# A decoder layer on one core: the input projection's twelve blocks in five groups, and w_o begun from its GLA half

## The chip, the core and the metric

The kernel runs on one core of one Trainium2 chip. The metric is device time in microseconds (us), the median of the runs shown; one profiled execution gives the trace. Five engines work side by side: TensorE (PE in the rows, with its weight loads as PEld), VectorE (DVE), ScalarE (ACT), GpSimd (POOL) and SyncE (SP), which here only issues the weight transfers.

## The reference

One layer, batch 1, 256 positions, width 2048, all in float32:

```python
c_act = jax.nn.silu(c)
mod = (c_act @ w_ada[l] + b_ada[l])[:, None, :]
sh1, sc1, gt1, sh2, sc2, gt2 = jnp.split(mod, N_MOD, axis=-1)
h = rms_norm(x, g_mix_norm[l]) * (1.0 + sc1) + sh1
proj = h @ w_in[l]
dq, dk, dv, gq, gk, gv, gg, g_low = jnp.split(proj, PROJ_SPLITS, axis=-1)
...
mix = jnp.concatenate([od, og], axis=-1) @ w_o[l]
x = x + gt1 * mix
h2 = rms_norm(x, g_ffn_norm[l]) * (1.0 + sc2) + sh2
u, g = jnp.split(h2 @ w_up[l], 2, axis=-1)
act = jax.nn.gelu(causal_dwconv(g, w_conv[l], b_conv[l]), approximate=False) * u
x = x + gt2 * (act @ w_down[l])
return rms_norm(x, g_final)
```

Between `proj` and `mix` stand two head groups: differential attention (DA, 8 heads, from dq, dk, dv) gives `od`, and gated linear attention (GLA, 4 heads, from gq, gk, gv, gg, with decays from g_low) gives `og`.

## The kernel before

**The stream of weights.** Every weight is read once, by SP, in transfers of 512 KB. A unit (`load_unit`, L97) is two k tiles of 128 rows by 512 columns: one transfer into a `raw` buffer, a rounding copy `wh` on ACT (L110), the remainder `wl` on DVE (L111). TensorE then does three products per tile, since float32 is made of two parts. `b_block` (L114) has the weights stationary, 24 matmuls of 256 columns per unit (recorded under L129); `a_block` (L149) has the activations stationary, 12 matmuls of 512 columns per unit (L163). There are five `raw` buffers, three `wh` and three `wl`.

**The modulation.** `c_act @ w_ada` is a product with one row. `ada_gen` (L207) loads w_ada through the same `raw` buffers (name `raw_a`), multiplies on DVE (`acc`, L241), adds up over partitions on TensorE (`ps_mod`, L221) and yields after each transfer. The generators wait in a list `bg`. Each `load_unit` adds `rate[0]` to a credit and takes one step of the list for every whole credit; `drain` takes steps until a named generator is done. In the list stand sh1 and sc1 (name ada1, eight generators of two k tiles each), then gt1, then sh2 and sc2 (ada2_0 to ada2_3), then gt2.

**The input projection.** Its 12 blocks of 512 columns are gk, gq, gv0, gv1, gg0, gg1, dq0, dk0, dv0 and dq1, dk1, dv1. The first nine are computed in groups of k tiles, `KGROUPS = (2, 4, 4, 6)`, since only those k tiles of h whose ada1 is done can be used: each group opens a block in PSUM (L723; a partial sum is copied back in by ACT, L726), adds its k tiles and closes it by an ACT copy (L731). `need` (L669) drains ada1 and forms h (`norm_T`) just ahead of the block that wants it. The last three blocks, `LATER`, run afterwards over all 16 k tiles at once. PSUM has two slots for blocks.

**The heads.** GLA and DA are generators too, in a second list `fg` with credits of its own, stepped by the units (`frate`). GLA starts behind gv1 of the last group, DA of heads 0 to 3 (`da(0)`) runs within LATER, DA of heads 4 to 7 (`da(1)`) within w_o.

**The output projection and beyond.** w_o has four blocks of 512 columns (nb). nb 0 and 1 take the GLA half of their rows first, then the DA rows; nb 2 and 3 take all rows. Then `drain("ada2_0")` (L818), the second norm, and the up projection in groups (4, 4, 8) of k tiles, seven of its eleven chunks spilled between groups. Then the down projection.

**The order.** The kernel is built with a scheduler that sorts each engine's instructions by a modelled timeline, within their dependences; engines and queues then run in that order.

Of the kernel before, what the change touches and what calls it, by code (L numbers as in the profile page):

```python
# [20 lines left out]
KGROUPS = (2, 4, 4, 6)  # L21
# [25 lines left out]
def tile_decoder_layer(  # L47
# [13 lines left out]
    RAW, WH, WL = 5, 3, 3  # L61
# [13 lines left out]
    fg, fcredit, frate = [], [0.0], [0.0]  # L75

# [20 lines left out]
    def load_unit(view, kt, c0):  # L97
# [8 lines left out]
        raw = stage.tile([P, 2, 512], F32, tag="raw", name="raw", bufs=RAW)  # L106
# [100 lines left out]
    def ada_gen(segs, width, c0, finish, psp, on_pe=(), by_rows=False):  # L207
# [122 lines left out]

    def setup_consts():
        dlam = t1.tile([P, 6, 64], F32, tag="w4", name="dlam", bufs=3)
        dl2 = dlam[:, 4:6]
# [23 lines left out]
        for h in range(DA_HEADS):  # L357
            V.tensor_scalar(identh[:, h], ident, 2.0 ** -(h + 1) / DA_SCALE, None, op0=ALU.mult)

        for l in range(NLEV + 2):  # L360
# [21 lines left out]
            V.tensor_copy(cmat[:, l], cf)  # L382

        for l in range(NLEV):
            h = 1 << l
# [281 lines left out]
    hT = []  # L667

    def need(kts):  # L669

        while len(hT) <= kts[-1]:
            k = len(hT)
            drain(ada1[k])
            hT.extend(norm_T(t1, rst1, s1, sh1, k, f"hT{k}", 1 if k == 0 else 2))

    def in_block(bi, ps, kts, first, last):
        n, c0, tr = BLOCKS[bi]
        need(kts)
        (b_block if tr else a_block)(ps, w_in_v, c0, kts, hT, first, last)
        if bi != 1:  # L680
            return
        if kts[0] == 0:
            setup_consts()
        pl = pss.tile([P, 512], F32, tag="ms", name="ps_low")
        for k in kts:
# [297 lines left out]
```

## Time and profile before

| | |
|---|---|
| median of 3 runs | 1324.97 us (1324.36 to 1326.58) |
| the profiled execution, its own time | 1323.78 us |
| its span in the trace | 1322.1 us |
| TensorE busy | 1247.1 us (94%), 8492 matmuls |
| VectorE busy | 898.2 us (68%) |
| ScalarE busy | 701.4 us (53%) |
| moved by DMA | 314.59 MB, mean 238 GB/s |

A busy TensorE is not one at its peak: a matmul's record is longer than the distance to the next one. So the work done in a stretch is counted by matmuls and their distance where they follow each other without a gap, and the rest of the stretch is loss.

### The profile page before, as it was taken

What the parts mean: (1) busy time and instruction counts of PE and PEld (TensorE: products, weight loads), DVE (VectorE), ACT (ScalarE), POOL (GpSimd) and SP (SyncE); (2) the same over time, 40 slices, a digit from 0 to 9 for tenths busy, and PEclk for the clock granted to TensorE, in tenths of its full rate; (3) what the DMA queues carried; (4) which work ended last, traced back from release to release, by engine and by line L of the source; (5) the groups of instructions that cost most, each with busy time, mean ns of one, the idle gap of its engine ahead of it and who ended that gap; (6) DMA issues with size and microseconds to landing.
All of it is one profiled execution on the core that took longest, in us unless ns stands there. A gap on an engine that the chain in (4) does not pass through costs nothing.

```text
span 1322.1 us, 21489 instructions
## 1 busy us (share of the span) xinstructions
PE 1247.1 (94%) x8492; PEld 1147.9 (87%) x8492; DVE 898.2 (68%) x1198; ACT 701.4 (53%) x914; POOL 30.4 (2%) x79
## 2 busy tenths in 40 slices
PE   4869889999999998799999999999999999999996
PEld 4658778899888998799999999999999988888885
DVE  4787787987666677768776687776666554545454
ACT  4546666674554543455767566654444443434343
POOL 1700000000000000000000000000000000000000
PEclk8879999999998999899999999999999999999998
DMA  8899999976466467889998777677777755555562
GB/s 273 272 300 299 300 301 315 305 254 204 144 190 206 145 209 254 283 293 315 318 332 278 232 230 234 208 220 232 224 229 232 243 188 191 194 194 195 181 205 98
DMA packets 172884, 314.59 MB, mean 238 GB/s; under 512 B 12813, under 2 KB 46285, under 8 KB 172782
## 3 DMA queue, kind: packets, MB, share of 16 engines
q1 hardware_dynamic: 168384, 307.28, 72.8%
q10 hardware_dynamic: 4398, 5.93, 1.3%
q8 instruction: 66, 1.08, 0.3%
q14 instruction: 36, 0.29, 0.1%
HBM read 311.07 MB, written 2.10 MB: 237 GB/s over the span
## 4 chain that ended last, share of the span: by engine, by line
PE 63%; DMA 20%; DVE 9%; issue 3%; ACT 2%; POOL 2%; SPq 0%; DVEq 0%; ACTq 0%; POOLq 0%
PE ps_h L129 27%; PE ps_d L163 18%; DMA raw_a<-in_w_ada_dram 14%; PE ps_o L129 5%; PE ps_mm L129 4%; DMA raw<-in_w_in_dram 4%; DVE acc L241 4%; DVE wl L111 3%; PE ps_mm L163 3%; DMA raw<-in_w_up_dram 2%; ACT wh L110 2%; PE ps_s L558 1%; DMA xtok<-in_x_dram 1%; PE ps_a L501 1%; PE ps_s L556 0%
## 5 line engine op out<-in xcount | busy, mean ns | idle before, releaser
L110 ACT ACTIVATE wh<-raw 128x1024 fp32r<-128x1024 f32 x392 | 414.3, 1058 | 462.7 <-PE ps_h L129 138.0
L111 DVE TENSOR_TENSOR wl<-raw,wh 128x1024 fp32r<-128x1024 f32 x392 | 478.5, 1223 | 253.5 <-ACT wh L110 250.6
L129 PE MATMUL ps_h<-h2T,wh 128*128 128x256 f32 x2816 | 511.2, 284 | 7.9 <-ACT h2T L277 6.7
L129 PEld LDWEIGHTS ps_h<-h2T,wh 128*128 128x128 f32 x2816 | 441.0, 193 | 8.9 <-ACT h2T L277 7.1
L129 PE MATMUL ps_h<-h2T,wl 128*128 128x256 f32 x1408 | 400.4, 285 | 4.8 <-DVE wl L111 4.7
L241 DVE SCALAR_TENSOR_TENSOR acc<-raw_a,cols,acc 128x512 f32<-128x512 f32 (+1 forms) x237 | 240.8, 1018 | 110.7 <-DMA raw_a<-in_w_ada_dram 106.2
L129 PEld LDWEIGHTS ps_h<-h2T,wl 128*128 128x128 f32 x1408 | 271.0, 193 | 6.8 <-DVE wl L111 6.7
L163 PE MATMUL ps_d<-wh,act 128*128 128x512 f32 x704 | 217.4, 389 | 0.8 <-DVE dx L941 0.8
L163 PEld LDWEIGHTS ps_d<-wh,act 128*128 128x128 f32 x704 | 132.2, 188 | 29.2 <-DVE dx L941 1.2
L129 PE MATMUL ps_mm<-hT,wh 128*128 128x256 f32 x768 | 146.9, 291 | 10.2 <-ACT hT L281 3.7
L163 PE MATMUL ps_d<-wl,act 128*128 128x512 f32 x352 | 137.8, 391 | 0.0
L129 PEld LDWEIGHTS ps_mm<-hT,wh 128*128 128x128 f32 x768 | 123.6, 197 | 13.8 <-ACT wh L110 4.1
L163 PE MATMUL ps_mm<-wh,hT 128*128 128x512 f32 x384 | 122.8, 394 | 2.8 <-ACT pj_gq L731 1.1
L129 PE MATMUL ps_mm<-hT,wl 128*128 128x256 f32 x384 | 111.9, 292 | 4.7 <-DVE wl L111 4.6
L129 PE MATMUL ps_o<-mixT,wh 128*128 128x256 f32 x512 | 97.6, 292 | 2.3 <-DVE xT L783 2.3
L163 PEld LDWEIGHTS ps_mm<-wh,hT 128*128 128x128 f32 x384 | 72.2, 188 | 19.8 <-ACT wh L110 1.8
L129 PEld LDWEIGHTS ps_o<-mixT,wh 128*128 128x128 f32 x512 | 82.7, 198 | 4.2 <-DVE xT L783 2.7
L163 PE MATMUL ps_mm<-wl,hT 128*128 128x512 f32 x192 | 77.2, 402 | 6.8 <-DVE wl L111 6.7
L129 PEld LDWEIGHTS ps_mm<-hT,wl 128*128 128x128 f32 x384 | 75.3, 196 | 6.5 <-DVE wl L111 6.1
L163 PEld LDWEIGHTS ps_d<-wl,act 128*128 128x128 f32 x352 | 66.1, 188 | 13.9 <-issue 0.5
L129 PE MATMUL ps_o<-mixT,wl 128*128 128x256 f32 x256 | 75.1, 293 | 1.5 <-DVE wl L111 1.5
L129 PEld LDWEIGHTS ps_o<-mixT,wl 128*128 128x128 f32 x256 | 50.8, 198 | 2.9 <-DVE wl L111 2.2
(237 smaller groups left out, 864.6 us busy)
## 6 DMA issues: line engine op xcount, KB each, us to landing
raw<-in_w_up_dram SPq DMA_DIRECT2D x176, 512.0 KB, 4.6
raw_a<-in_w_ada_dram SPq DMA_DIRECT2D x128, 512.0 KB, 5.0
raw<-in_w_in_dram SPq DMA_DIRECT2D x96, 512.0 KB, 5.5
raw<-in_w_down_dram SPq DMA_DIRECT2D x88, 512.0 KB, 4.5
raw_a<-in_w_ada_dram SPq DMA_DIRECT2D x128, 256.0 KB, 4.7
raw<-in_w_o_dram SPq DMA_DIRECT2D x32, 512.0 KB, 4.4
xtok<-in_x_dram ACTq DMA_DIRECT2D x4, 512.0 KB, 10.1
gfin<-in_g_final_dram ACTq DMA_DIRECT2D x2, 512.0 KB
```

The costliest lines, as they stand in the source:

```text
L110: A.activation(h, raw, AF.Copy)
L111: V.tensor_tensor(l, raw, h, op=ALU.subtract)
L129: PE.matmul(ps[:, m * T:(m + 1) * T], w[:, j, ms], xt[k][:, xx, :], start=(first and k == kts[0] and m % 2 == 0 and i == 0), stop=(last an ...
L163: PE.matmul(ps[:, tb * 512:(tb + 1) * 512], xt[k][:, xx, tsl], w[:, j, :], start=(first and k == kts[0] and i == 0), stop=(last and k == k ...
L241: V.scalar_tensor_tensor(acc, raw[:, j], col, acc, op0=ALU.mult, op1=ALU.add)
L501: PE.matmul(pv[:, i, tb], lhs, rhs, start=True, stop=True)
L558: PE.matmul(pv, q[rs, hb * T + tb * P:hb * T + (tb + 1) * P], k[rs, hb * T:hb * T + n], start=False, stop=(tb == 1), skip_group_check=True)
```

## The change

- `KGROUPS` becomes (2, 2, 4, 4, 4), and each group is taken by all twelve blocks; only in group 4 (the fourth) are dq1, dk1, dv1 left out, and they take eight k tiles in the last group.
- The order of blocks turns round from group to group (`ORDER`), so that the last two blocks of a group stay in PSUM and are the first two of the next; they are not copied out and in.
- ada1 has one generator per group (256 columns of each of two parts for the first two groups, 512 for the other three), and forming h is a generator step (`norm_gen`) behind it in the list, so that it is paced by the units; `drain(f"norm{g}")` stands ahead of each group.
- The rates per unit are 0.95, 1.65, 0.85, 1.1, 0.8 for the groups (before 1.2, and 1.0 in the last), 0.9 in w_o (before 0.3, as in LATER), 0.75 in the first two up groups (before 1.05), 0.27 after (before 0.25).
- There are 8 `raw` buffers up to the second norm, and 5 after it.
- `setup_consts` yields and is stepped once per unit from the third group on; the g_low product runs once, in the last group, after its first two units.
- GLA's tiles `W` take slots of the pool that holds h (freed ones) in place of their own.
- da(0) starts behind dv0 of the last group, da(1) behind the whole projection.
- w_o: nb 0 and 1 take the GLA half and are spilled by ACT copies, nb 2 and 3 take the GLA half and stay in PSUM; then the DA heads must be done, nb 2 and 3 are finished, and nb 0 and 1 are copied in and finished.

The core of the diff:

```diff
-KGROUPS = (2, 4, 4, 6)
+KGROUPS = (2, 2, 4, 4, 4)
-R_K, R_LAST, R_LATER, R_WO, R_SP, R_UP = 1.2, 1.0, 0.3, 0.3, 1.05, 0.25
-F_GLA, F_DA0, F_DA1 = 2.2, 1.5, 1.6
+R_K, R_WO, R_SP, R_UP = (0.95, 1.65, 0.85, 1.1, 0.8), 0.9, 0.75, 0.27
+F_GLA, F_DA = 2.0, 1.7
-    RAW, WH, WL = 5, 3, 3
+    WH, WL = 3, 3
+    rawp, RAW = [p1.enter_context(tc.tile_pool(name="raw1", bufs=1))], [8]
...
-        if hd % 2 == 0:
-            W = [t1.tile([P, 4, NTB, P], F32, tag=f"W{i}", name=f"W{i}") for i in range(2)]
+        if hd < 2:
+            Wt.append([ktp.tile([P, 4, NTB, P], F32, tag="kt", name=f"W{hd}{i}") for i in range(2)])
...
+    def norm_gen(kts):
+        for k in kts[::2]:
+            hT.extend(norm_T(t1, rst1, s1, sh1, k, f"hT{k}", 1 if k == 0 else 2))
+            yield
+    for g, kts in enumerate(KG):
+        n, k0 = len(kts), kts[0]
+        bg.append(("ada1", ada_gen((0, 1), n * P, k0 * P, mod_cols(s1, sh1, 0, GM, k0, n), get_ps,
+                                   FIRST_PE if g == 0 else ())))
+        bg.append((f"norm{g}", norm_gen(kts)))
...
+    forth = GLA_BLOCKS + DA1_BLOCKS + DA0_BLOCKS
+    ORDER = [forth, forth[::-1], forth, (GLA_BLOCKS + DA0_BLOCKS)[::-1],
+             ("gq", "gk") + GLA_BLOCKS[2:] + DA0_BLOCKS + DA1_BLOCKS]
...
     for g, kts in enumerate(KG):
         last = g == len(KG) - 1
+        drain(f"norm{g}")
+        rate[0] = R_K[g]
...
+        for n in order[2:]:
+            in_part(n, KG[g - 1] + kts if last and n in DA1_BLOCKS else kts)
+            if last or n not in order[-2:]:
+                close(n, last)
+    while len(fg) > 1:
+        fstep()
     for hd in range(GLA_HEADS):
         gla_T(hd)
     fg.append(da(1))
...
     po = [psm.tile([P, 1024], F32, tag="mm", name="ps_o") for _ in range(2)]
+    for nb in range(2):
+        wo_part(nb, po[nb], 0, 8)
+        spo.append(prj.tile([P, 1024], F32, tag=("pj_gk", "pj_gq")[nb], name=f"spill_o{nb}"))
+        A.activation(spo[nb], po[nb], AF.Copy)
+    po += [psm.tile([P, 1024], F32, tag="mm", name="ps_o") for _ in range(2)]
     for a, b in ((0, 8), (8, 12), (12, 16)):
+        if a == 8:
+            while len(fg) > 1:
+                fstep()
+            for hp in range(2):
+                da_T(hp)
+        if a == 12:
+            fdrain()
+            drain("gt1")
+        for nb in (2, 3):
             wo_part(nb, po[nb], a, b)
```

What it moves, at the places that matter. **SP's queue** in the middle of the second group, before: `raw` is a weight unit of w_in, `raw_a` a transfer of w_ada (two parts of 256 columns, so two transfers make one step).

```order
L107 DMA raw<-in_w_in_dram 128x2x512 x2
L231 DMA raw_a<-in_w_ada_dram 128x2x256 x2
L107 DMA raw<-in_w_in_dram 128x2x512
L231 DMA raw_a<-in_w_ada_dram 128x2x256 x2
L107 DMA raw<-in_w_in_dram 128x2x512
L231 DMA raw_a<-in_w_ada_dram 128x2x256 x2
L107 DMA raw<-in_w_in_dram 128x2x512
L231 DMA raw_a<-in_w_ada_dram 128x2x256 x4
```

And now, from the end of the first group on:

```order
L235 DMA raw_a<-in_w_ada_dram 128x2x256 x2
L111 DMA raw<-in_w_in_dram 128x2x512 x3
L232 DMA raw_a<-in_w_ada_dram 128x2x512
L111 DMA raw<-in_w_in_dram 128x2x512
L232 DMA raw_a<-in_w_ada_dram 128x2x512
L111 DMA raw<-in_w_in_dram 128x2x512
L232 DMA raw_a<-in_w_ada_dram 128x2x512 x2
L111 DMA raw<-in_w_in_dram 128x2x512
```

The transfers of w_ada are wide from here on. In the queue before, 128 narrow and 17 wide ones stand ahead of the 66th weight unit; now it is 32 narrow and 53 wide.

**TensorE's queue** where the first DA head begins, before: `ps_s` are its scores, and behind them come rows of the block dk1 (L129). The transposes `ps_pd` of the same head stand 57 matmuls further on.

```order
L556 LDWEIGHTS identh
L556 MATMUL ps_s_3210<-causal,identh 128x256
L558 MATMUL ps_s_3210<-pj_dk_146,pj_dq_145 128x256
L129 MATMUL ps_mm<-hT_1430,wh 128x256 x2
L129 MATMUL ps_mm<-hT_1430,wl 128x256
L129 MATMUL ps_mm<-hT_1933,wh 128x256 x2
L129 MATMUL ps_mm<-hT_1933,wl 128x256
```

Now, at the seam between the last projection block and w_o:

```order
L564 LDWEIGHTS identh
L564 MATMUL ps_s_3624<-causal,identh 128x256
L566 MATMUL ps_s_3624<-pj_dk_150,pj_dq_149 128x256
L594 MATMUL ps_pd<-ident,pt 128x128
L564 LDWEIGHTS identh
L564 MATMUL ps_s_3676<-causal,identh 128x128
```

The transpose stands right behind the scores, with no block between. Further down the same seam the GLA transposes `ps_t` and the first matmul of w_o follow:

```order
L594 MATMUL ps_pd<-ident,pt 128x128 x2
L600 MATMUL ps_od<-pj_dv_151,pdT 128x128
L601 MATMUL ps_od<-pj_dv_151,pdT 128x128
L602 MATMUL ps_od<-pj_dv_151,pdT 128x128
L547 MATMUL ps_t<-ident,pj_gg_147 128x128 x8
L547 MATMUL ps_t<-ident,pj_gg_148 128x128 x4
L133 MATMUL ps_o<-mixT_3719,wh 128x256
```

Before, the rows of `ps_t` stood among the matmuls of dv1.

**VectorE's queue** in the middle of w_o's first half, now: `acc` of the modulation (L245) stands between the steps of a DA head (`st`, `pt`, `ods`), with `wl` of the units.

```order
L266 TENSOR_TENSOR gt_90<-ps_mod,bcol 128x8
L245 SCALAR_TENSOR_TENSOR acc<-raw_a,cols,acc 128x1024
L570 TENSOR_REDUCE st<-ps_s_3974 128x1 x2
L115 TENSOR_TENSOR wl<-raw,wh 128x1024
L571 TENSOR_SCALAR st<-st 128x2
L570 TENSOR_REDUCE st<-ps_s_3975 128x1 x2
L245 SCALAR_TENSOR_TENSOR acc<-raw_a,cols,acc 128x1024
L571 TENSOR_SCALAR st<-st 128x2
```

And before, for a DA head within w_o:

```order
L111 TENSOR_TENSOR wl<-raw,wh 128x1024 x2
L562 TENSOR_REDUCE st<-ps_s_4099 128x1 x2
L563 TENSOR_SCALAR st<-st 128x2
L241 SCALAR_TENSOR_TENSOR acc<-raw_a,cols,acc 128x1024
L562 TENSOR_REDUCE st<-ps_s_4100 128x1 x2
L563 TENSOR_SCALAR st<-st 128x2
L111 TENSOR_TENSOR wl<-raw,wh 128x1024
```

One head had one or no `acc` among its steps; now it has two.

## Rows read from the trace of the kernel before

**Rows 1.** The page: span, busy time of each engine with its share, then TensorE's busy share, the granted clock and the DMA share in 40 slices of the span.

```profile
span 1322.1 us, 21489 instructions
...
PE 1247.1 (94%) x8492; PEld 1147.9 (87%) x8492; DVE 898.2 (68%) x1198; ACT 701.4 (53%) x914; POOL 30.4 (2%) x79
...
PE   4869889999999998799999999999999999999996
...
PEclk8879999999998999899999999999999999999998
DMA  8899999976466467889998777677777755555562
```

**Rows 2.** Windows, two that hold only one kind of matmul: L129 (256 columns) in the up projection, L163 (512 columns) in the down projection. Columns: stretch, its length, TensorE busy with the number of records, weight loads, granted clock, DMA share, GB/s.

```profile
740.00:1000.00 260.00, 259.42 (x2157) 258.82 (x2156) 1.00 0.75 226
...
1100.00:1200.00 100.00, 100.00 (x443) 82.80 (x442) 1.00 0.58 189
```

**Rows 3.** Windows by stage, all instructions. Columns: stretch, length, busy of PE, PEld, DVE, ACT, POOL with numbers, granted clock, DMA share, GB/s.

```profile
0.00:240.00 240.00, 194.23 (x1125) 167.60 (x1125) 179.47 (x279) 143.64 (x177) 30.43 (x79) 0.94 0.93 296
240.00:520.00 280.00, 277.62 (x1937) 252.66 (x1938) 204.38 (x390) 147.95 (x282) 0.00 (x0) 0.99 0.65 204
520.00:540.00 20.00, 10.46 (x66) 9.26 (x65) 18.42 (x28) 7.46 (x12) 0.00 (x0) 0.83 0.98 338
540.00:700.00 160.00, 154.16 (x1244) 151.90 (x1245) 116.37 (x113) 96.81 (x110) 0.00 (x0) 0.98 0.90 305
```

**Rows 4.** The same windows for one line alone: first L129 in all four, then L163 in the two in which it occurs.

```profile
0.00:240.00 240.00, 85.45 (x624) 81.05 (x624) 0.94 0.93 296
240.00:520.00 280.00, 162.21 (x1256) 155.59 (x1257) 0.99 0.65 204
520.00:540.00 20.00, 7.00 (x44) 6.30 (x43) 0.83 0.98 338
540.00:700.00 160.00, 149.58 (x1192) 146.42 (x1193) 0.98 0.90 305
...
0.00:240.00 240.00, 82.66 (x337) 61.73 (x337) 0.94 0.93 296
240.00:520.00 280.00, 58.59 (x239) 43.72 (x239) 0.99 0.65 204
```

**Rows 5.** Windows of the first stage, all instructions: the first 100 us, the rest up to 140 us more, and a piece in which the DMA share is highest.

```profile
0.00:100.00 100.00, 65.07 (x351) 57.01 (x352) 69.89 (x138) 50.16 (x71) 30.43 (x79) 0.85 0.91 281
100.00:240.00 140.00, 129.16 (x775) 110.59 (x774) 109.58 (x142) 93.48 (x107) 0.00 (x0) 1.00 0.95 307
80.00:100.00 20.00, 11.32 (x62) 10.55 (x62) 16.18 (x25) 8.81 (x11) 0.00 (x0) 0.66 0.99 310
```

**Rows 6.** Timeline of TensorE: the first matmul of the projection, then, at a block's first matmul in the first group, the wait for the copy that closes the block before. Columns: start, duration, engine, line, operation, and in brackets the idle time ahead and what ended it.

```profile
35.27 0.58 PE L129 MATMUL ps_mm<-hT,wh 128*128 128x256 f32 x1 [1.02 <-ACT wh L110]
...
45.96 0.50 PE L163 MATMUL ps_mm<-wh,hT 128*128 128x512 f32 x1 [0.65 <-ACT pj_gk L731]
...
50.04 0.50 PE L163 MATMUL ps_mm<-wh,hT 128*128 128x512 f32 x1 [1.07 <-ACT pj_gq L731]
```

**Rows 7.** VectorE's groups by form: number, busy time, mean ns, and idle time ahead with its releaser; then VectorE's windows of 240 to 520 us for `wl` alone and for `acc` alone.

```profile
L241 DVE SCALAR_TENSOR_TENSOR acc<-raw_a,cols,acc 128x1024 f32<-128x1024 f32 x120 | 153.8, 1282 | 88.0 <-DMA raw_a<-in_w_ada_dram 88.0
...
240.00:520.00 280.00, 88.03 (x73) 0.99 0.65 204
...
240.00:520.00 280.00, 44.40 (x35) 0.99 0.65 204
```

**Rows 8.** Two windows where VectorE is fullest, all instructions.

```profile
240.00:260.00 20.00, 19.44 (x99) 16.65 (x100) 20.00 (x39) 13.00 (x17) 0.00 (x0) 1.00 0.90 283
260.00:300.00 40.00, 40.00 (x284) 37.54 (x283) 34.48 (x67) 27.07 (x36) 0.00 (x0) 1.00 0.82 266
```

**Rows 9.** Timeline around the first DA head: the head's last scores on TensorE, the step of VectorE that releases its transposes, the ACT copy of a transposed result (of the next row on), and VectorE's part of a transposed GLA head.

```profile
337.85 0.70 PE L558 MATMUL ps_s<-pj_dk,pj_dq 64*128 64x256 f32 x2
...
341.71 0.75 DVE L583 SCALAR_TENSOR_TENSOR pt<-pt,st 128x128 f32<-128x128 f32 x2
...
346.56 0.49 ACT L588 ACTIVATE pdT<-ps_pd 128x384 f32<-128x384 f32 x1 [0.73 <-PE ps_pd L586]
...
400.34 0.68 DVE L444 TENSOR_TENSOR mixT<-ps_t,mixT 128x512 fp32r<-128x512 f32 x1
```

**Rows 10.** A window behind small matmuls at the start of w_o, all instructions: the granted clock is the third number from the end.

```profile
410.00:418.00 8.00, 8.00 (x37) 7.10 (x37) 3.92 (x8) 1.44 (x3) 0.00 (x0) 0.57 0.62 213
```

**Rows 11.** Timeline from w_o into the up projection: SP's run of eight w_ada transfers, VectorE waiting for one, a small matmul group, and TensorE's first matmul of the up projection.

```profile
508.98 13.00 SPq L228 DMA_DIRECT2D raw_a<-in_w_ada_dram  x8
...
513.93 1.28 DVE L241 SCALAR_TENSOR_TENSOR acc<-raw_a,cols,acc 128x1024 f32<-128x1024 f32 x1 [3.06 <-DMA raw_a<-in_w_ada_dram]
...
530.34 1.84 PE L221 MATMUL ps_mod<-ones,acc 128*128 128x1 f32 x16
...
539.83 0.80 PE L129 MATMUL ps_h<-h2T,wh 128*128 128x256 f32 x2 [6.68 <-ACT h2T L277]
```

More of the change, by code (lines that the diff above doesn't have):

```diff
@@ L395, in setup_consts @@
             V.tensor_copy(masks[:, l], mf)
+            yield
     BLOCKS = [
@@ L665, in da @@
                 yield
[L667 to L685, printed above, removed]
-            for xx in range(2):
-                PE.matmul(pl[0:32, 0:T], wlow2[:, k, :], hT[k][:, xx, :],
-                          start=(k == kts[0] and xx == 0), stop=(k == kts[-1] and xx == 1))
-        if kts[0] == 0:
-            A.activation(lowT[0:32], pl[0:32, 0:T], AF.Copy)
-        else:
-            V.tensor_tensor(lowT[0:32], pl[0:32, 0:T], lowT[0:32], op=ALU.add)
     steps(5)
@@ new lines, in tile_decoder_layer, with in_part @@
+    forth = GLA_BLOCKS + DA1_BLOCKS + DA0_BLOCKS
+    ORDER = [forth, forth[::-1], forth, (GLA_BLOCKS + DA0_BLOCKS)[::-1],
+             ("gq", "gk") + GLA_BLOCKS[2:] + DA0_BLOCKS + DA1_BLOCKS]
+    COLS = {n: (c0, tr) for n, c0, tr in BLOCKS}
+    where = {}
+    def in_part(n, kts):
+        if n not in where:
+            where[n] = psm.tile([P, 1024], F32, tag="mm", name="ps_mm")
+            if kts[0]:
+                A.activation(where[n], pj[n], AF.Copy)
+        c0, tr = COLS[n]
+        (b_block if tr else a_block)(where[n], w_in_v, c0, kts, hT, kts[0] == 0, False)
@@ L719, in tile_decoder_layer, with close @@
+    def close(n, last):
+        A.activation(pj[n], where.pop(n), AF.Copy)
+        if not last:
+            return
+        if n == "gk":
+            log_decay()
+        if n == "gv1":
+            fg.append(gla())
+            frate[0] = F_GLA
+        if n == "gg1":
+            silu_gates()
+            gates_ready.append(1)
+        if n == "dv0":
+            fg.append(da(0))
     for g, kts in enumerate(KG):
         last = g == len(KG) - 1
-        rate[0] = R_LAST if last else R_K
@@ L743, in tile_decoder_layer @@
+        rate[0] = R_K[g]
+        if g == 2:
+            setup.append(setup_consts())
+        if g == len(KG) - 2:
+            nc.scalar.dma_start(out=wlow, in_=w_in_v[:, :, C_LOW:C_LOW + 16])
+        if last:
+            setup_low()
+        order = ORDER[g]
+        lead = order[:2]
         halves = [kts[i:i + 2] for i in range(0, len(kts), 2)]
-        lead = [open_block(bi) for bi in range(2)]
         for i, ks in enumerate(halves):
-            for bi in range(2):
-                in_block(bi, lead[bi], ks, g == 0 and i == 0, i == len(halves) - 1)
+            for n in lead:
+                in_part(n, ks)
@@ L774, in tile_decoder_layer @@
-    drain("gt1")
+    frate[0] = F_DA
     KO = list(range(8, 16)) + list(range(0, 8))
+    NB_ORDER = (2, 3, 0, 1)
+    K_ENDS = [4 * nb + m for nb in NB_ORDER for m in range(4)]
     sqs = t1.tile([P, T], F32, tag="odq", name="sqs", bufs=1)
```

133 lines of the change are left out of this document (53 added, 80 removed).

## The prediction

> **What bounds the kernel now.** I read the page's 40 slices first [rows 1]: TensorE is at its fullest from the tenth slice to the end, with one dent, while DMA is at 8 or 9 tenths only in the first nine slices and again around the dent. So the limit changes by stage. A busy TensorE says little, so I count matmuls. Where nothing disturbs them, 2157 matmuls of 256 columns take 259.4 us, 0.1203 us each, and 443 of 512 columns take 100 us, 0.2257 us each [rows 2]. A unit of weights is then 24 x 0.1203 = 2.89 us in a `b_block` and 12 x 0.2257 = 2.71 us in an `a_block`. Small matmuls outside the GLA and DA heads go at about 0.115 us (16 in 1.84 us [rows 11]).
>
> Stage by stage [rows 3, 4]:
> - 0 to 240 us: 624 x 0.1203 + 337 x 0.2257 + 164 others x 0.115 = 75 + 76 + 19 = 170 us of work, 70 us lost. DMA share 0.93: this stage waits for weights. In units, 624/24 + 337/12 = 54 of the 96 of w_in are done.
> - 240 to 520 us: TensorE busy 277.6 of 280. Large matmuls make 1256 x 0.1203 + 239 x 0.2257 = 205 us, so the 442 small ones of the heads fill the other 72.6 us. Little is lost.
> - 520 to 540 us: 44 x 0.1203 + 22 x 0.115 = 7.8 us of work, 12.2 lost.
> - 540 to 700 us: 1192 x 0.1203 + 52 x 0.115 = 149.4 us, 10.6 lost, of which 3 by the clock (0.98).
>
> Behind 700 us the change alters nothing but a rate (0.25 to 0.27) under a full TensorE, which I cost at nothing: a transfer more is hidden by the DMA slack of the slices there. What can be won is thus some 90 us of loss, of which the start (no projection matmul before 35.3 us [rows 6]) stays.
>
> **The change part by part.** A gain is +, in us.
>
> **A. The projection in five groups of twelve blocks: +25.** The idea is that TensorE gets more work per byte of w_ada. In the queue before, 128 narrow and 17 wide transfers of w_ada stand ahead of the 66th unit, now 32 and 53: 42.5 MB have become 36.2 MB, and with 66 units of 0.524 MB and 2.7 MB on ACT's queue this makes 73.5 MB instead of 79.8. When is the 66th unit through TensorE? By DMA: 28.1 MB in the first 100 us (281 GB/s) and the other 45.4 MB at 307 GB/s [rows 5] give 248 us. The narrow transfers are also dear: with them the engines carried 310 GB/s at a share of 0.99, with wide ones alone 338 at 0.98 [rows 5, 3], 313 and 345 GB/s at a full share. At 345 x 0.95 the 45.4 MB take 138 us, so 238 us. The eight buffers instead of five help to hold that share. By TensorE: 35.3 us, 33 units of each kind = 184.7 us, some 12 us of small matmuls and clock at the start: 232 us. I take 245 us, half way between the two DMA times and 2 us for the last unit. By then TensorE has done 184.7 + 136 x 0.115 = 200 us of work (the g_low products come later), where before it had done 170 + 5 = 175 at 245 us. The difference is 25, and each us of delay takes one away. Bounds: +38 (232 us) and +14 (256 us, the second rival).
>
> On narrow transfers the Trainium skill (DMA: Bandwidth & Descriptors, "Why small descriptors are slow (HBM only)") gives a fixed overhead of about 3 cycles per packet beside one cycle per 32 bytes. From that figure, 1 KB rows cost 35/32 and 2 KB rows 67/64, an estimate of 4.5% between them, where the trace has 10%. By the page the DMA time would be some 246 us in place of 238 and the term about 4 us smaller.
>
> What it adds: the blocks are opened and closed more often, 49 + 37 copies by ACT where 36 + 27 and three more stood, about 20 copies of 1.02 us, and two spills with their return in w_o. ACT is busy 144 of 240 us in this stage [rows 3], so it has room; the price would be TensorE waiting for the copy at a block's start, 0.65 to 1.07 us in the first group [rows 6]. While weights are late, that wait is inside the wait for weights. The constants (POOL and DVE) leave the first 60 us and are spread over the third group; the W tiles in freed slots and the turn of order cost nothing, since the last readers of those slots are two groups back.
>
> **B. A fuller VectorE from there to the end of w_o: -5.** Of 204.4 us of VectorE in 240 to 520 us, 73 `wl` took 88.0 and 35 `acc` 44.4 [rows 3, 7]; 72 us are heads and rest. Now 62 units stand there (74.8 us) and 50 w_ada transfers, 47 of them on VectorE (47 x 1.27 = 59.7 us): 206.5 us in all. TensorE has 48 units of 2.89, 14 of 2.71 and 75.8 us of small matmuls: 252 us. VectorE would be at 82%, and more while heads run. At 86% TensorE lost nothing; at 100% it lost 0.56 us of 20 [rows 8], which is 7 us over 252. I take 5, between 0 and 12.
>
> **C. The seam between projection and w_o: -8.** Before, three blocks covered the end of GLA and the first DA heads. Now the scores of the first head are followed at once by its own transposes. From the end of the scores (338.55) to the end of VectorE's step (342.46) it took 3.9 us [rows 9]; nothing fills that. Then 0.6 us for the ACT copy, some 1.8 us until VectorE's part of the first GLA head (0.68 us, queued behind the second head's steps) releases w_o, and half a chance that the clock falls as it did behind small matmuls, 0.57 for 8 us [rows 10], 3.4 us: 3.9 + 0.6 + 1.8 + 1.7 = 8. Bounds 4 and 13.
>
> **D. The end of da(1) within w_o: -3.** The last head's scores have about 1.1 us of other work behind them in TensorE's queue, against the same 3.9 us. 0 to 5.
>
> **E. The clock at the old start of w_o: +3** (0 to 3.4): the drop at 410 to 418 us [rows 10] stood behind a row of small matmuls that are now elsewhere.
>
> **F. Into the up projection: +4.** Before, w_o ended with eight w_ada transfers in a row; VectorE waited up to 3.1 us for one, and the last `wl` and sums stood behind it [rows 11]. With 0.9 steps per unit, ada2_0 is done before w_o ends. What stays is the chain through the norm, 6.7 us [rows 11]. Of 12.2 lost, some 8 remain. 0 to 5.
>
> **G. The first two up groups: +4.** At 0.75 steps per unit, 0.92 MB go with 2.89 us of matmuls, 318 GB/s, less than the 345 a full share gives; before, 1.05 steps needed more. About four steps are left to drain at the end of the second group. Of 10.6 lost, 7 can go; I take 4, 0 to 7.
>
> **The sum:** 25 - 5 - 8 - 3 + 3 + 4 + 4 = +20. The span of 1322.1 becomes 1302, the profiled execution's 1323.8 becomes 1304, and the median of 1325.0, which is 1.2 above that execution, **1305 us**.
>
> **The rivals.**
>
> *TensorE runs at its own limit throughout.* If the wide transfers and eight buffers put DMA ahead of TensorE, A is +38 and B nothing: 20 + 13 + 5 = 38, **1287 us**. For it: DMA and TensorE are only 6 us apart at the better rate. Against it: the share already stood at 0.95 to 0.99, so the engines, not the buffers, set the rate.
>
> The Trainium skill (Perfetto Trace Analysis, "Roofline") lets one active core pull up to about 435 GB/s. Taken as reachable here, it would make this rival the rule; no row comes nearer than 345 GB/s at a full share.
>
> *The block switches come to light.* In the first three groups about 30 blocks start behind an ACT copy in front of TensorE. At 0.8 us each [rows 6] this is 24 us, 256 us for A, +14; with B at 7 the sum is 7: **1318 us**. It decides where weights are on time.
>
> *VectorE waits in line and takes the gain back.* Its queue is in order: an `acc` whose transfer has not landed holds all behind it, `wl` and the DA steps. Before, 120 wide `acc` waited 88.0 us, 0.73 us each [rows 7], 3.1 us at worst in [rows 11]. In the stage of B, 47 such waits of 0.73 add 34 us: 241 of TensorE's 252. At 1.5 us each VectorE needs 277 and the gain is gone; at 1.7 it needs 286, 34 more than TensorE, 29 worse than my 5: **1335 us**. For it: there are 47 `acc` where 35 stood, between DA steps. Against it: DMA has slack there, and eight buffers let transfers run ahead.
>
> That the scheduler undoes the order is not a case: the queues show the twelve blocks and the steps as written.
>
> **How the numbers follow.** The forecast has 0.55 (1296 to 1314), the first rival 0.12, the second 0.19, the third 0.14. About 0.2%, 2.6 us, is what a measurement of this kernel can tell from no change. Faster than that: 0.55, 0.12 and most of the second, 0.83; slower: most of the third, 0.11; 0.06 between. The bounds of the terms, added as squares (12, 6, 4.5, 2.5, 2, 3, 4), make 15 us either way; the range 1290 to 1321 leaves out most of the third rival and half of the first.
>
> **What would show it.** For A, some 66 units done at 245 us, GB/s over 315 from 100 us on, and no dip of the clock below 0.9 there. For B, TensorE busy over 95% until w_o ends, with `acc` waiting under 1 us in the mean. For C and D, a gap of 3 to 4 us ahead of the first `ps_pd`, and one of 2 to 3 us ahead of the last. For F, one wait of 6 to 7 us ahead of `ps_h` and no run of w_ada transfers. It is wrong if the 66th unit comes after 260 us, or if the stage of B takes over 285 us.

## The result and the profile after

| | median | runs | ratio to the kernel before |
|---|---|---|---|
| kernel before | 1324.66 us | 4 (1322.15 to 1326.58) | |
| changed kernel | 1338.07 us | 4 (1336.48 to 1341.03) | 1.0105, 95% interval 1.0079 to 1.0130 |

The change costs 13 us, 1%, where 20 us of gain were forecast. The profiled execution took 1341.03 us, its span is 17.2 us longer than that of [rows 1]. The page of the changed kernel: span, busy times, TensorE's busy share, granted clock and DMA share in 40 slices, and of the chain that ended last the shares by engine.

```profile
span 1339.3 us, 21357 instructions
...
PE 1252.1 (93%) x8492; PEld 1156.0 (86%) x8492; DVE 887.6 (66%) x1137; ACT 723.5 (54%) x937; POOL 30.6 (2%) x79
...
PE   4798999989979989789999999999999999999996
...
PEclk8899999989969989799999999999999999999999
DMA  9899999867744653778879777767777765665662
...
PE 69%; DMA 14%; DVE 7%; ACT 4%; issue 3%; POOL 2%; SPq 0%; ACTq 0%; DVEq 0%
```

The first stage is fuller than before, as forecast; the dents now lie in the middle, in the 9th, 12th, 15th, 17th and 18th slice, where [rows 1] has two low slices in a row. The chain holds 14% of DMA, of which 13 are transfers of w_ada (in the kernel before 20 and 14, so this share alone tells nothing of the loss).

To see which term went wrong, work is counted stage by stage, as in the prediction: 0.1203 us for each matmul of 256 columns, 0.2257 for each of 512, and for a small one 0.115 up to 240 us and 0.15 behind, a value between that and the 0.164 which the heads took in the prediction. The rest of the stage is loss; where it comes out below 0, the price of a small matmul was too high. Three stages of the changed kernel, first all of TensorE, then L133 (the `b_block` matmul, L129 before), then L167 (the `a_block`, L163 before):

```profile
240.00:300.00 60.00, 54.87 (x320) 0.94 0.75 239
...
360.00:400.00 40.00, 31.27 (x130) 0.72 0.50 165
...
560.00:720.00 160.00, 148.91 (x1209) 0.99 0.80 261
...
240.00:300.00 60.00, 21.31 (x168) 20.38 (x168) 0.94 0.75 239
...
240.00:300.00 60.00, 26.22 (x96) 19.12 (x96) 0.94 0.75 239
360.00:400.00 40.00, 9.82 (x41) 7.18 (x39) 0.72 0.50 165
```

From 240 to 300 us, 168 x 0.1203 + 96 x 0.2257 + 56 x 0.15 = 50.3 us of work: 9.7 lost. From 360 to 400 there are 41 large matmuls and 89 small ones, 22.6 us: 17 lost, with the granted clock at 0.72. Done so for every stage, beside the terms of the prediction (the last two columns are the first experiment). The stages were counted in pieces of 20 to 60 us and added up; a matmul across an edge counts twice, so the losses of the longer stages stand some tenths, at most about 1 us, too low, and the differences are hardly touched:

| term, stage | loss before | loss after | forecast | came | loss in `acc_behind` | gain there |
|---|---|---|---|---|---|---|
| A, 0 to 240 | 69.1 | 44.3 | +25 | +24.8 | 46.0 | +23.1 |
| B, 240 to 360 and 480 to 500 | 0.8 | 9.7 | -5 | -8.9 | -2.6 | +3.4 |
| C, seam, 360 to 400 | -1.0 | 17.0 | -8 | -18.0 | 8.0 | -9.0 |
| D and E, 400 to 480 | 5.6 | 9.7 | 0 | -4.1 | 8.7 | -3.1 |
| F, into up, 500 to 560 | 16.2 | 17.2 | +4 | -1.0 | 14.0 | +2.2 |
| G, up groups, 560 to 720 | 3.8 | 12.9 | +4 | -9.1 | -1.5 | +5.3 |
| sum | | | +20 | -16.3 | | +21.9 |

A came as forecast. The 24.8 us it gains are given back behind 240 us, in B, C and G above all. VectorE's and ACT's sums of w_ada (`acc`), by form, which answer to [rows 7]:

```profile
L245 DVE SCALAR_TENSOR_TENSOR acc<-raw_a,cols,acc 128x1024 f32<-128x1024 f32 x165 | 211.7, 1283 | 147.4 <-DMA raw_a<-in_w_ada_dram 146.1 <-ACT acc L243 1.2
...
L243 ACT ACTIVATE acc<-raw_a,cols 128x1024 f32<-128x1024 f32 x11 | 12.6, 1149 | 21.7 <-DMA raw_a<-in_w_ada_dram 21.7
```

Each of VectorE's waits 0.89 us in the mean, before 0.73. That alone explains little; one of them, on the timeline, shows how time is lost. VectorE around the wait, then ACT's `wh` and SP's issue ahead of it, and TensorE's next matmul that needs a `wl`:

```profile
265.85 1.28 DVE L245 SCALAR_TENSOR_TENSOR acc<-raw_a,cols,acc 128x1024 f32<-128x1024 f32 x1 [1.13 <-DMA raw_a<-in_w_ada_dram]
267.05 1.22 DVE L115 TENSOR_TENSOR wl<-raw,wh 128x1024 fp32r<-128x1024 f32 x1
268.18 0.68 DVE L441 TENSOR_SCALAR lsm<-ps_z 128x512 f32<-128x512 f32 x1
272.79 1.28 DVE L245 SCALAR_TENSOR_TENSOR acc<-raw_a,cols,acc 128x1024 f32<-128x1024 f32 x1 [3.92 <-DMA raw_a<-in_w_ada_dram]
273.99 0.69 DVE L444 TENSOR_TENSOR lsm<-lsm,lse 128x512 f32<-128x512 f32 x1
274.59 1.22 DVE L115 TENSOR_TENSOR wl<-raw,wh 128x1024 fp32r<-128x1024 f32 x1
...
265.74 1.06 ACT L114 ACTIVATE wh<-raw 128x1024 fp32r<-128x1024 f32 x1
...
267.16 0.34 SPq L232 DMA_DIRECT2D raw_a<-in_w_ada_dram  x1
...
275.86 0.80 PE L167 MATMUL ps_mm<-wl,hT 128*128 128x512 f32 x1 [4.46 <-DVE wl L115]
```

The `wl` at 274.59 is the 74th and belongs to the 74th `wh`, done at 266.8. It stood behind a sum whose transfer SP had issued only at 267.16, just after the sum before had ended (265.85 + 1.28) and freed its buffer. Six of the other seven held units, loaded or on their way, whose `wl` stood behind the sum too. TensorE stood still for 4.46 us, and from 275 to 282 us the granted clock was 0.51: the matmul behind the wait took 0.80 us, those ahead of it 0.39 to 0.40. The Trainium skill (PSUM — Partial Sum Buffer, "Engine vs sequencer instructions") calls the queues of ScalarE, VectorE and GpSimd strict FIFO; the trace agrees: the `wl`, whose `wh` was ready, started 7.8 us later, behind another `wl`, two short steps and the sum with its wait of 3.92 us.

The order of the queues shows how common this is. For each wide sum on VectorE, placed by the `wl` ahead of it, I count the units that SP loads ahead of its transfer and whose `wl` stands behind it:

| sums between units | before, 5 buffers | changed, 8 buffers |
|---|---|---|
| 64 and 125 | 1 to 4, mean 2.7 | 5 to 7, mean 5.6 |
| 126 and 183 | 0 to 3, mean 0.8 | 0 to 4, mean 1.8 |

In the mean, 2.4 of eight buffers were left to run ahead, and 2.3 of five.

### The profile page after: what moved, and what is told of

Its sections match the earlier page's. It is cut to its first block, busy times and chain, and to the rows that moved or that the text cites. A ratio compares the mean times of both kernels' runs of the same rounds, so it can differ in the third digit from the quotient of the medians.

```text
span 1339.3 us, 21357 instructions
## 1 busy us (share of the span) xinstructions
PE 1252.1 (93%) x8492; PEld 1156.0 (86%) x8492; DVE 887.6 (66%) x1137; ACT 723.5 (54%) x937; POOL 30.6 (2%) x79
## 4 chain that ended last, share of the span: by engine, by line
PE 69%; DMA 14%; DVE 7%; ACT 4%; issue 3%; POOL 2%; SPq 0%; ACTq 0%; DVEq 0%
PE ps_h L133 32%; PE ps_d L167 18%; DMA raw_a<-in_w_ada_dram 13%; PE ps_mm L167 7%; PE ps_mm L133 5%; PE ps_o L133 4%; DVE wl L115 3%; DVE acc L245 2%; ACT wh L114 1%; PE ps_s L566 1%; DMA raw<-in_w_up_dram 1%; DVE W L484 1%; ACT ps_mm L730 1%; PE ps_mod L225 1%; DVE at L514 0%
## 5 line engine op out<-in xcount | busy, mean ns | idle before, releaser
L133 PE MATMUL ps_h<-h2T,wh 128*128 128x256 f32 x2816 | 514.0, 285 | 8.1 <-ACT h2T L281 5.9
L133 PEld LDWEIGHTS ps_h<-h2T,wh 128*128 128x128 f32 x2816 | 442.9, 194 | 9.0 <-ACT h2T L281 6.3
L133 PE MATMUL ps_h<-h2T,wl 128*128 128x256 f32 x1408 | 402.1, 286 | 11.3 <-DVE wl L115 11.3
L245 DVE SCALAR_TENSOR_TENSOR acc<-raw_a,cols,acc 128x1024 f32<-128x1024 f32 (+1 forms) x192 | 231.8, 1208 | 153.7 <-DMA raw_a<-in_w_ada_dram 152.1
L133 PEld LDWEIGHTS ps_h<-h2T,wl 128*128 128x128 f32 x1408 | 272.2, 193 | 13.7 <-DVE wl L115 13.6
L167 PE MATMUL ps_d<-wh,act 128*128 128x512 f32 x704 | 217.3, 389 | 0.8 <-DVE dx L964 0.8
L167 PEld LDWEIGHTS ps_d<-wh,act 128*128 128x128 f32 x704 | 132.2, 188 | 29.2 <-DVE dx L964 1.2
L133 PE MATMUL ps_mm<-hT,wh 128*128 128x256 f32 x768 | 145.0, 289 | 11.5 <-ACT hT L281 4.4
L167 PE MATMUL ps_d<-wl,act 128*128 128x512 f32 x352 | 137.8, 391 | 0.0
L133 PEld LDWEIGHTS ps_mm<-hT,wh 128*128 128x128 f32 x768 | 123.7, 196 | 13.5 <-ACT ps_mm L730 5.1
L167 PE MATMUL ps_mm<-wh,hT 128*128 128x512 f32 x384 | 125.7, 398 | 1.9 <-ACT pj_gq L735 1.4
L133 PE MATMUL ps_mm<-hT,wl 128*128 128x256 f32 x384 | 110.7, 288 | 0.7 <-DVE wl L115 0.7
L133 PE MATMUL ps_o<-mixT,wh 128*128 128x256 f32 x512 | 97.9, 291 | 2.8 <-ACT ps_o L837 1.8
L167 PEld LDWEIGHTS ps_mm<-wh,hT 128*128 128x128 f32 x384 | 73.0, 191 | 18.5 <-ACT pj_gq L735 1.8
L133 PEld LDWEIGHTS ps_o<-mixT,wh 128*128 128x128 f32 x512 | 81.7, 195 | 4.8 <-ACT ps_o L837 1.9
L167 PE MATMUL ps_mm<-wl,hT 128*128 128x512 f32 x192 | 76.4, 398 | 4.5 <-DVE wl L115 4.5
L167 PEld LDWEIGHTS ps_d<-wl,act 128*128 128x128 f32 x352 | 66.1, 188 | 13.9 <-issue 0.5
L133 PEld LDWEIGHTS ps_mm<-hT,wl 128*128 128x128 f32 x384 | 75.3, 196 | 1.1 <-DVE wl L115 1.1
L133 PE MATMUL ps_o<-mixT,wl 128*128 128x256 f32 x256 | 73.3, 287 | 0.0
L133 PEld LDWEIGHTS ps_o<-mixT,wl 128*128 128x128 f32 x256 | 49.7, 194 | 0.4 <-issue 0.3
```

Source lines behind the costliest of these rows:

```text
L133: PE.matmul(ps[:, m * T:(m + 1) * T], w[:, j, ms], xt[k][:, xx, :], start=(first and k == kts[0] and m % 2 == 0 and i == 0), stop=(last an ...
L167: PE.matmul(ps[:, tb * 512:(tb + 1) * 512], xt[k][:, xx, tsl], w[:, j, :], start=(first and k == kts[0] and i == 0), stop=(last and k == k ...
L245: V.scalar_tensor_tensor(acc, raw[:, j], col, acc, op0=ALU.mult, op1=ALU.add)
```

## The experiments

**Theory 1**: sums stand at the head of VectorE's and ACT's queue ahead of loaded units, and wait there for transfers that these units hold back. **Theory 2**: the time goes at the seam, where heads stand with no other matmuls between. **Rival 3**: the transfers are the limit; more are asked for than DMA carries.

Twelve kernels ran, in rounds with the kernel before, which took 1321.7 to 1321.8 us then; the changed kernel's ratio makes 1335.6 us on that scale. Differences below are taken from ratios. Line numbers in rows are those of the kernel shown.

### acc_behind: every sum behind the unit ahead of it

```diff
+    def queued(ws):
+        return tc.issue_after(ws[-1 - BACK]) if len(ws) > BACK else ExitStack()
...
-        A.activation(h, raw, AF.Copy)
-        V.tensor_tensor(l, raw, h, op=ALU.subtract)
+        whs.append(A.activation(h, raw, AF.Copy).ins)
+        wls.append(V.tensor_tensor(l, raw, h, op=ALU.subtract).ins)
...
-                    A.activation(acc, raw[:, j], AF.Copy, scale=col)
+                    with queued(whs):
+                        A.activation(acc, raw[:, j], AF.Copy, scale=col)
                 else:
-                    V.scalar_tensor_tensor(acc, raw[:, j], col, acc, op0=ALU.mult, op1=ALU.add)
+                    with queued(wls):
+                        V.scalar_tensor_tensor(acc, raw[:, j], col, acc, op0=ALU.mult, op1=ALU.add)
```

`issue_after` binds only the order of issue on that engine; BACK is 0.

> The changed kernel, with one thing added: each sum of a w_ada transfer (`acc`, on VectorE and the first of a row on ACT) is queued behind the `wl` (or `wh`) of the weight unit that was loaded just before it. In the changed kernel the 60 sums between the 64th and the 125th unit stand on VectorE ahead of 5 to 7 `wl` whose units were loaded earlier, with 8 buffers in all. Theory 1 (the sums wait at the head of VectorE's and ACT's queue for a transfer that cannot be issued until the units behind them are used): the 9 us lost at 240 to 300 us go, the wait of 7.2 us of ACT ahead of its first sum at 369 us too, and some 5 of the 12 us lost from 560 to 740: 1316 to 1323 us; `acc` waits under 0.4 us in the mean where it was 0.89. Theory 2 (the time went at the seam, where DA heads stand with no other matmuls between) alone: 1335 to 1338. Rival 3 (the transfers themselves are the limit, too many bytes are asked for after 240 us): 1338, and the waits are found on `wl` instead.

Measured: **1302.19 us**, ratio 0.9845 (0.9825 to 0.9866), 34 us less than the changed kernel. The sums by form, and TensorE in two stages:

```profile
L251 DVE SCALAR_TENSOR_TENSOR acc<-raw_a,cols,acc 128x1024 f32<-128x1024 f32 x165 | 211.2, 1280 | 2.2 <-DMA raw_a<-in_w_ada_dram 1.8
...
L248 ACT ACTIVATE acc<-raw_a,cols 128x1024 f32<-128x1024 f32 x11 | 12.6, 1142 | 3.5 <-DMA raw_a<-in_w_ada_dram 3.5
...
240.00:300.00 60.00, 60.00 (x395) 1.00 0.83 277
...
560.00:720.00 160.00, 159.10 (x1318) 0.99 0.86 289
```

147 us of waits became 2.2, and VectorE was not slower for it. Its idle time did not vanish: ahead of `wl` it rose from 231 to 310 us, nearly all of it for ACT's `wh`. 240 to 300 us and the up groups are full, at more GB/s than in the changed kernel (277 for 239, 289 for 261): the transfers were not the limit, rival 3 falls. The gain is larger than theory 1 had expected (13 to 20 us): half of the seam's loss went too, and all of that in the up groups.

### seam and seam_behind: the first DA heads behind w_o's first unit

```diff
-        if n == "dv0":
-            fg.append(da(0))
...
+        if nb == 0:
+            wo_part(0, po[0], 0, 2)
+            hold.append([i for i in nc.cur_bb.bb.instructions if i.engine == mybir.EngineType.PE][-1])
+            fg.extend((da(0), da(1)))
-        wo_part(nb, po[nb], 0, 8)
+        wo_part(nb, po[nb], 0 if nb else 2, 8)
```

with each later step of the heads under `issue_after(hold[0])`; `seam_behind` has the edit of the first run as well.

> The changed kernel, with one thing changed: the first four DA heads are handed out only after the first unit of w_o, and their matmuls are queued behind it, so that the projection's end, the last GLA head, its transposes and w_o follow one another. Theory 2 (the 17 us lost at 360 to 400 us are DA heads in a row with nothing between, and the clock that falls with them): 10 to 13 us less, 1325 to 1328. Theory 1 (sums in line hold up VectorE wherever the heads stand): the waits move with the heads into w_o, 1332 to 1338.

Measured: 1333.52 us, ratio 1.0085 (1.0066 to 1.0104), hardly told from the changed kernel and within theory 1's range. The seam's loss fell from 17.0 to 9.0 us, and in the two profiled executions that was not given back (103.3 us lost up to 720 us, for 110.9). But that of the changed kernel (1341.03 us) is the slowest of its four; by the medians some 3 us were won, which the intervals don't tell from nothing.

> Both edits at once. If both theories hold, their gains add up, since the one is mostly at 240 to 300 and 560 to 740 us and the other at 360 to 400: 1303 to 1314 us. If theory 1 is the cause at the seam too (ACT's wait of 7.2 us delays the last GLA head, which delays the heads), the gains overlap: 1314 to 1320, no better than the first edit alone by more than 4 us.

Measured: 1307.70 us, ratio 0.9894 (0.9876 to 0.9912), 6 us slower than the sums' edit alone; the seam's loss is 7.8 us in the one and 8.0 in the other. Theory 2 falls as the main cause: with the sums in line, taking the heads out of the seam gives nothing, and w_o's end pays for it (8.0 lost at 480 to 500 us, for 0.2).

### before_behind: the sums' edit in the kernel before

> The kernel before, with the sums queued behind the preceding unit's `wl` as in the first run. There 2 to 4 of 5 buffers held units behind a sum in the seam, w_o and up, and 0 to 2 elsewhere. Theory 1: 3 to 6 us of the 7 lost in the up groups and of the small losses in w_o go, 1319 to 1322. Rival 3 (the transfers are the limit): 1325, no change.

Measured: 1318.62 us, ratio 0.9976 (0.9964 to 0.9989). The size is what theory 1 had forecast, and the kernel before had only 3 us to give. The place is so in part: in the two profiled executions 3.8 us less are lost before 240 us and 3.5 less from 540 to 700, but 2.8 more from 400 to 480.

### behind_first and behind_wo: the edit in one half of the kernel

`queued` works only while a flag is set, which turns where w_o begins to be handed out.

> The changed kernel with the sums queued behind the preceding unit only where they are handed out before w_o begins (the projection with GLA). Theory 1 has 36 us to share out: 9 us lost at 240 to 300, and of the 17 at the seam what ACT's wait of 7.2 us and the waits ahead of it made, 5 to 10: 1319 to 1325 us. If the gain comes from the start of the kernel (the first 240 us) instead, nothing of it is left here to find elsewhere: 1302.

Measured: 1328.62 us, ratio 1.0048 (1.0027 to 1.0069): 7.5 us less, not 11 to 17. The 240 to 300 us are full (-0.2 lost), but the seam still loses 16.2.

> The counterpart: the sums queued behind the preceding unit only from w_o on (w_o, the up groups and what follows). Theory 1: 12 us at 560 to 740, 6 at the end of the DA heads, some at the way into up: 16 to 22 us less than the changed kernel, 1316 to 1322, and together with the run before it the whole 36.

Measured: 1306.72 us, ratio 0.9871 (0.9837 to 0.9904): 31 us less, more than expected. Here the seam loses 4.0 us and the up groups none. Together the two halves make 38 us, the 34 of the whole within the intervals, but the share of the seam was put in the wrong half: the sums that hold it up are handed out with w_o and float ahead of its units, into the seam.

### behind4: a sum ahead of at most four units

BACK is 4 in place of 0.

> The dose between: each sum may stand ahead of at most 4 units loaded before it (the first run: none; the changed kernel: 5 to 7 between the 64th and the 125th unit, at most 4 elsewhere). So only the stretch of 240 to 480 us is altered. Theory 1: with 4 of 8 buffers free to run ahead, 2.1 MB or some 6 us of transfers against 5.2 us from issue to landing, about half the waits there go: 1318 to 1328. If any place ahead of loaded units is as bad as another: 1335 to 1340.

Measured: 1323.93 us, ratio 0.9998 (0.9976 to 1.0020), 14 us less, as theory 1 had it. 240 to 300 us lose 0.1 where 9.7 went, the seam 11.5 for 17.0; the up groups are unaltered (16.0 lost, 12.9 in the changed kernel).

### five_behind: five buffers in place of eight

> The first run (all sums behind the preceding unit), with 5 raw buffers in the projection where the changed kernel has 8. Theory 1: a buffer holds nothing back once the sums stand in the order of the transfers; five are 2.6 MB, 7.7 us of transfers at 340 GB/s, over the 5.2 us to landing: 1302 to 1306. If the eight buffers are what makes the first 240 us fuller: 1310 to 1316, lost before 240 us.

Measured: 1313.58 us, ratio 0.9917 (0.9885 to 0.9949), 9.5 us slower than with eight: theory 1's number was missed, the eight buffers do something of their own. It is lost before 240 us (54.5 for 46.0). The stretch that shows it, 60 to 120 us (TensorE, granted clock, DMA share, GB/s), first with five buffers, then with eight:

```profile
60.00:120.00 60.00, 52.30 (x315) 0.97 0.93 312
```

```profile
60.00:120.00 60.00, 55.24 (x344) 0.95 1.02 370
```

### dve_only and act_only: the edit on one engine

Only the one or the other `with queued(...)` stands.

> The first run's edit for VectorE's sums alone; the first sum of each row, 11 on ACT, stands where the changed kernel has it. Theory 1 says the place on either queue counts by what waits behind it: 154 of the waits, 147 us, are VectorE's, 22 us ACT's, of which 7.2 at the seam: 1302 to 1310. If it was ACT's one wait that made the seam's 17 us: 1311 to 1320.

Measured: 1310.92 us, ratio 0.9915 (0.9899 to 0.9932), 25 us less, a little over the range. That is on the edge between the two ranges; by stages both are right, since 240 to 300 us lose only 0.8 and the up groups 1.6, but the seam still loses 15.4. Its rows, ACT, VectorE and TensorE:

```profile
372.15 1.15 ACT L247 ACTIVATE acc<-raw_a,cols 128x1024 f32<-128x1024 f32 x1 [2.85 <-DMA raw_a<-in_w_ada_dram]
...
376.54 1.23 DVE L116 TENSOR_TENSOR wl<-raw,wh 128x1024 fp32r<-128x1024 f32 x1 [4.15 <-ACT wh L115]
...
379.91 0.45 PE L599 MATMUL ps_pd<-ident,pt 128*128 128x128 f32 x1 [7.96 <-DVE pt L596]
```

A sum on ACT waits, so a `wh` is late, so VectorE stands at its `wl`, so the head's step behind it is late, and TensorE waits 8 us. Of these, 2.85 are the wait for the transfer; the rest is work of ACT and VectorE that stands in line between. In the changed kernel the same place reads so (ACT, then TensorE twice):

```profile
369.38 1.15 ACT L243 ACTIVATE acc<-raw_a,cols 128x1024 f32<-128x1024 f32 x1 [7.19 <-DMA raw_a<-in_w_ada_dram]
...
378.43 1.19 PE L523 MATMUL ps_o<-pj_gv,at 128*128 128x256 f32 x2 [4.01 <-DVE at L514]
...
390.19 0.45 PE L594 MATMUL ps_pd<-ident,pt 128*128 128x128 f32 x1 [4.14 <-DVE pt L591]
```

> The counterpart: only ACT's 11 first sums are queued behind the preceding unit. Theory 1: VectorE's 147 us of waits stay, so 1328 to 1336. If ACT's wait at the seam is the cause there: 1318 to 1327.

Measured: 1310.86 us, ratio 0.9918 (0.9903 to 0.9933), 25 us less: far below both ranges. The seam loses 4.6 us, 240 to 300 us nothing, the up groups 1.7; only the end of the heads in w_o is worse (11.8 at 440 to 480). VectorE's sums still wait, 0.65 us each in the mean:

```profile
L250 DVE SCALAR_TENSOR_TENSOR acc<-raw_a,cols,acc 128x1024 f32<-128x1024 f32 x165 | 211.5, 1282 | 107.8 <-DMA raw_a<-in_w_ada_dram 107.0
```

So theory 1 had the place right and the price wrong: the waits' total is no measure of what they cost. Where they stand says more. Of all VectorE's waits for w_ada, 55 us here and 57 in the changed kernel lie before 240 us or behind 720, where TensorE lacks weights or is full anyway; from 240 to 300 us they fell from 14.0 to 5.2 us, and the loss there from 9.7 to nothing. The 11 sums on ACT are each the first of a row, and VectorE's 15 others of the row follow it; with the first in line the row starts in line (1 unit behind it) and only drifts ahead (up to 5 or 6) by its end. In the up groups VectorE waits for sums, then TensorE for `wl`, in the changed kernel and here:

```profile
DVE acc L245 <- DMA raw_a<-in_w_ada_dram: 47.4, 27, 4.1
...
PE ps_h L133 <- DVE wl L115: 11.0, 7, 3.8
```

```profile
DVE acc L250 <- DMA raw_a<-in_w_ada_dram: 30.0, 21, 3.6
...
PE ps_h L134 <- DVE wl L116: 2.3, 3, 1.5
```

A third fewer waits on the one engine, four fifths less on the other. There are three `wl` buffers, so my reading is that TensorE feels only what exceeds what they hold; no run varies their number.

### best3 and best4: what is left in w_o

Each pair of DA heads gets its transposes as soon as it is done, with F_DA 2.0; in `best4` BACK is 4 up to w_o, 0 from there.

```diff
-            if b and i and i % 2 == 0:
+            if i and i % 2 == 0:
...
-            for hp in range(2):
-                da_T(hp)
```

> The first run's edit, and in w_o each pair of DA heads handed its transposes as soon as it is done (in the first run they come all at the ninth unit pair of w_o, where TensorE waited 3.8 us for VectorE and the clock fell to 0.88), with 2.0 steps of the heads per unit for 1.7. The 8.9 us lost at 400 to 460 us in the first run become about 4: 1296 to 1299 us. If the chain of the heads is the limit and not its place: 1302.

Measured: 1305.34 us, ratio 0.9876 (0.9860 to 0.9891); no gain, rather 4 us worse than `acc_behind`. 400 to 480 us lost 7.7 for 8.7, 480 to 520 lost 10.3 for 6.7: the wait moved to the end of w_o.

> As the run before, but in the projection a sum may stand ahead of up to 4 loaded units (from w_o on of none). With that freedom the run with the edit from w_o on alone lost 4 us at the seam where the first run lost 8: 1292 to 1297 us. If the seam's difference between those two runs is the profile's scatter: the same as the run before.

Measured: 1305.12 us, ratio 0.9874 (0.9858 to 0.9890). The seam's loss did fall, to 5.0 us, and the time did not. So `acc_behind`, the change with its sums in line, has the lowest median of the kernels, 1.5% under the kernel before and 2.6% under the change as it was made; the intervals of `behind_wo`, `best3` and `best4` overlap with its own.

## Why the prediction was wrong

- **A held in its size, and in part by luck.** +24.8 for +25, 63.4 units done at 240 us (706 matmuls of 256 columns, 408 of 512), 325 GB/s over the stage for 296 [rows 3], the clock at 0.97 or more from 60 us on. The block switches (second rival) did not come to light: 0.3 us lost from 120 to 240. `five_behind` puts 8.5 us of the 23 to 25 on the eight buffers, which the prediction had used as a help to hold the share and not priced. Its reason against the first rival, that "the engines, not the buffers, set the rate", is refuted by the same run (312 GB/s with five, 370 with eight). Nor are narrow transfers dear by their short rows as such: from 60 to 120 us of the kernel before, packets of 1 KB took 50.4 ns in the mean and those of 2 KB among them 103.2, nearly the same per byte, while 2 KB took 92.1 in the changed kernel. So the 10% that the prediction read between two stretches is no price of row length alone; what slowed both sizes stays open.
- **The step that failed** is one sentence: "That the scheduler undoes the order is not a case: the queues show the twelve blocks and the steps as written." They do for blocks and steps, but not for the sums. In term B I counted only that there are 47 where 35 stood and let the wait of 0.73 us [rows 7] vanish in VectorE's slack; from 241 to 280 us it was 1.6 us in the mean of eight. B came to -8.9 for -5, C to -18.0 for -8, G to -9.1 for +4. Whose `wl` stands behind each sum could have been read from the order before the run: 5.6 in the mean, for 2.7.
- **"Against it: ... eight buffers let transfers run ahead"** was the reason that made the third rival small, and it was wrong as the kernel stood: the three more buffers went to units that waited behind the sum.
- **The third rival was right in its mechanism, and by its sum in one stretch only.** It added waits to VectorE's work until VectorE becomes the bound, from 1.5 us a wait. From 241 to 280 us that is what happened: VectorE's busy time and its waits for w_ada (us, times, longest), 1.6 us each in the mean, fill 38.9 of 39 us, and TensorE loses 8.9 us there:

```profile
241.00:280.00 39.00, 26.04 (x26) 0.94 0.80 258
...
DVE acc L245 <- DMA raw_a<-in_w_ada_dram: 12.9, 8, 3.9
```

  Over 240 to 520 us the two make 242 of 280 us (198.69 and 43.6), and yet 36 us were lost from 240 to 500 us: VectorE need not be full for its waits to cost time. The rival put its 29 us into the stage of B alone, where 8.9 were lost; that its time (1335 us, by its own sum 1334) fits is luck. What seems to decide is whether one wait is longer than the matmuls in hand (the row at 275.86 us), and whether a wait on ACT and one on VectorE stand behind each other (`dve_only`, `act_only`).
- **B, C, F and G** left out what stands behind a waiting sum, and in `acc_behind`, where nothing does, the sum comes out: +21.9 for +20, 1302 us for the forecast 1305. F and G are +7.5 for +8. The rest fits in part by luck: B is +3.4 for -5, with VectorE at 78% (218.50 of 280 us from 240 to 520), and makes up for D and E (-3.1 for 0) and A. C is -9.0 for -8, but not by its mechanism. The gap ahead of the first `ps_pd`, 3.9 us of the forecast 8, is 0.78:

```profile
370.56 0.30 PE L600 MATMUL ps_pd<-ident,pt 128*128 128x128 f32 x1 [0.78 <-DVE pt L597]
```

  TensorE is idle for 2.2 of the 40 us there, and the granted clock is 0.87, which makes 5.2 us where the prediction had 1.7.
- **What stays open**: why ACT's edit alone clears the up groups, where VectorE's order is nearly that of the changed kernel (1.5 units behind a sum in the mean of 126 to 183, for 1.8). Either edit alone brings their loss from 12.9 us under 2; no run parts the two within one row. And what a better way from w_o into the up projection could give: 14 us are lost at 500 to 560 us in `acc_behind`, 16.2 in the kernel before, on the chain through the norm.
- **A slip that changes nothing**: DMA is at 8 or 9 tenths in the first eight slices of [rows 1], not in the first nine.

## What to carry to other kernels

Where a scheduler sorts queues by a modelled timeline, read for each instruction that waits for a DMA how many loaded buffers are used behind it: the buffers that are left are what can run ahead (2.4 of eight here, 2.3 of five). Such side work belongs behind the use of the load ahead of it, on every engine that shares the buffers, and binding the order was worth 34 us here, where the change itself moved 13. Waits are not to be priced by their sum over the kernel: look at the stage in which they stand, at the longest, and at what the engine behind has in hand.

## What was not expected of the hardware

- The DMA engines carried more than the prediction's 345 GB/s at a full share. One window of the changed kernel, TensorE, clock, share and GB/s:

```profile
80.00:100.00 20.00, 19.65 (x132) 1.00 1.05 386
```

  Per full share that is 368 GB/s, and 60 to 120 us of `acc_behind` had 370 at 1.02 (the share adds up the time of all packets, so it can pass 1). The Trainium skill (Perfetto Trace Analysis, "Roofline") has about 435 GB/s as the bound of one core's 16 DMA engines; the highest 20 us of any run here, 201 to 221 us of `dve_only`, have 389.
- At the seam the granted clock fell to its lower level, 1.2 GHz, within TensorE's wait of 4.01 us that ends at 378.43, and stayed there through the second wait and the small matmuls between, up to 401 us. Windows of TensorE, granted clock, DMA share and GB/s:

```profile
376.00:380.00 4.00, 1.57 (x4) 0.69 0.68 211
...
384.00:388.00 4.00, 2.05 (x5) 0.50 0.68 249
...
396.00:400.00 4.00, 3.43 (x16) 0.50 0.04 16
```

  The two matmuls of `ps_o` at 378.43 us have 1.19 us there; in `acc_behind`, at the higher level, the same two take half:

```profile
362.87 0.60 PE L529 MATMUL ps_o<-pj_gv,at 128*128 128x256 f32 x2
```

  So this wait of 4 us cost more than 4.
